# A trunk layer on one core: half steps in a fixed order per engine, and inner down projections in seven products

## The chip, the cores and the metric

One core of a Trainium2 chip runs the whole kernel in one launch. The metric is the device time of a run in microseconds (us); lower is better. TensorE (PE) multiplies, VectorE (DVE) and GpSimd (POOL) work elementwise, ScalarE (ACT) applies functions and copies, and SyncE (SP) issues all DMAs.

## The reference

One layer is run for 128 context tokens and 512 latent tokens (640 columns here) of width 1024, in fp32:

```
h = mod(rms_norm(x));  x += 1/2 * gate1 * (silu(h @ w_gate) * (h @ w_up)) @ w_down     (half step 1, d_ff 2816)
h = mod(rms_norm(x));  x += gate2 * ((g_a * fourier(h) + g_b * gla(h)) @ w_out)        (mixer)
h = mod(rms_norm(x));  x += 1/2 * gate3 * (silu(h @ w_gate) * (h @ w_up)) @ w_down     (half step 2)
```

The shifts, scales and gates come from silu(c) @ w_ada, with 9 x 1024 columns. The outputs are the normed x and the final states of the attention branch.

## The kernel before, in words

Activations lie with channels on the partitions, in pages of 128 x 2 x 640 (`page`, 29 buffers). For precision each operand of a large matmul is split in a high and a low part (`split`, lines 108 to 110: ACT copies the high part, DVE subtracts it for the low part), and each product is three matmuls (high x high, high x low, low x high).

A pair of output tiles (256 columns of a weight, all 640 tokens) is computed either plainly (`gemm_w`, 96 matmuls of 128 x 128 by 320 columns for 8 row tiles) or as a 2 x 2 block product with seven half-size products instead of eight (`Pair7`, 84 matmuls). `Pair7` needs sums of weight blocks, made by POOL in place (lines 522, 523, 538, 539), and sums of activation blocks, made once per activation (`Act7`). Its weights are split two blocks at a time (`double`, 1024 columns, for products 1+2, 7+5 and 6+3) and one alone (`single`, 512 columns, for product 4):

```
            if i in (1, 2):
                self.double(self.raw[:, :, 0:P], 1, 2, whole)
            elif i in (5, 7):
                self.weights(1)
                self.sums7()
                self.double(self.raw[:, self.ks[0], :], 7, 5, lambda j, o: (j, o * P))
```

Products 1, 2, 6, 5 and 7 of a pair run in `begin` and `end`; products 3 and 4 are held back (`held`) and run inside the next pair. What is done with a finished bank is a `Take` object's: `p1` and `p2` read the banks of products 1 and 2, `p16` reads the sum of 1 and 6, and so on.

A half step (`ffn`, lines 650 to 731) goes through the 22 hidden tiles in `PARTS` of 4, 6, 6 and 6: for each two hidden tiles f there is a gate pair and an up pair; after the first gate pair of the next part come the down projections of the part that is finished (`down`, plain, 8 output tiles; line 378 adds them to X). The last part's down projection runs in two halves of the tokens (`halved`, lines 382 to 424), so that the next norm, or the output, can begin. The first two hidden tiles are made plainly at the entry; the gate pair of the third and fourth is the first `Pair7`. In half step 1 the parts of w_ada for later stages are streamed in (`ada_stream`, 14 steps of four 512 KB loads and one small product each, `ada_fill` between pairs).

The program is traced in order, and a scheduler then orders each engine's instructions by a cost model of its own, within the dependencies. `pin(start)` (line 58) forbids that: it ties each instruction to the one before it on its engine. Before, the entry of a half step is pinned; the pairs after it are not. Buffers: `wraw` 2 (raw weights, 1 MB), `wspl2` 4 blocks of 1024 columns, `wspl` 2 blocks of 512, PSUM 6 banks for products. In the mixer, the gates (columns C_G of w_in), the Fourier inputs (C_F) and w_proj_gla are also `Pair7` pairs.

Of the kernel before, what the change touches and what calls it, by code (L numbers as in the profile page):

```python
# [34 lines left out]
def trunk_kernel(ctx: ExitStack, tc: tile.TileContext, I, O):  # L35
# [6 lines left out]
    wspl2 = ctx.enter_context(tc.tile_pool(name="wspl2", bufs=NBLK2))  # L42
# [54 lines left out]
    def sm_tile(shape, tag, dt=F32):  # L97
        uid[0] += 1
        return small.tile(shape, dt, tag=tag, name=f"{tag}{uid[0]}")
# [16 lines left out]
    def block2():  # L116
        uid[0] += 1
        return wspl2.tile([P, 2, 1024], F32R, tag="wspl2", name=f"wsplb{uid[0]}")

    def wsplit(src, new=block2, room=1024):  # L120
# [194 lines left out]
    class Norm:  # L315
# [27 lines left out]
        def spread(self, hf):  # L343
            rb = sm_tile([P, N], "t")[0:GB, 0:NG * P].rearrange("p (g c) -> p g c", g=NG)
# [36 lines left out]
    def halved(wd, r0, nk, acts, gate, X, each, mid, cut=NH):  # L381
# [22 lines left out]
        for hf, c0, c1 in ((0, 0, cut), (1, cut, N)):  # L404
            opened = []
            for mp in range(4):
                rd = load(wd, r0, nk, mp * 256, 256)
                for m in range(2):
                    w = wsplit(rd[:, :, m * P:(m + 1) * P])
                    ps = pb_ps()  # L410
                    if hf == 0 and mp < 2:
                        some(ps, w, c0, c1, range(nk - 2))
                        opened.append((2 * mp + m, ps, w))
                        flush_pair()
                        continue
# [8 lines left out]
    def even(h):  # L424
        return h[:, :, 0:NH]
# [51 lines left out]
    held = []  # L477

    def flush_step():
        if held:  # L480
            held.pop(0)()

    def flush_pair():
        while held:
            flush_step()

    class Pair7:
# [3 lines left out]

        def __init__(self, raw, act, take, alternate=False):
            n = self.n = raw.shape[1] // 2
            ks = (slice(0, 2 * n, 2), slice(1, 2 * n, 2)) if alternate else (slice(0, n), slice(n, 2 * n))
            self.ks, self.raw = ks, raw
            self.a11, self.a12, self.a21, self.a22 = [raw[:, k, c:c + P] for c in (0, P) for k in ks]
            self.act, self.take = act, take
            self.w, self.summed = {}, False

        def double(self, src, a, b, at):  # L500
            t = block2()[:, :, 0:2 * self.n * P]
            k, c = src.shape[1], src.shape[2]
# [12 lines left out]
        def early(self):
            self.single(1, self.a11)
            self.single(2, self.a12)
            self.sums7()

        def sums7(self):  # L520
            if not self.summed:
                G.tensor_tensor(out=self.a11, in0=self.a11, in1=self.a21, op=ALU.subtract)  # L522
                G.tensor_tensor(out=self.a21, in0=self.a21, in1=self.a22, op=ALU.add)  # L523
                self.summed = True

        def weights(self, i):
            if i in self.w:
                return
            whole = lambda j, o: (range(2 * self.n)[self.ks[o]][j], 0)
            if i in (1, 2):  # L530
                self.double(self.raw[:, :, 0:P], 1, 2, whole)
            elif i in (5, 7):
                self.weights(1)
                self.sums7()
                self.double(self.raw[:, self.ks[0], :], 7, 5, lambda j, o: (j, o * P))
            elif i in (6, 3):
                self.weights(7)
                G.tensor_tensor(out=self.a11, in0=self.a22, in1=self.a11, op=ALU.subtract)  # L538
# [930 lines left out]
```

## Time and profile before

| | |
|---|---|
| median of 3 runs | 1606.99 us (1605.3 to 1608.22) |
| profiled execution | 1608.41 us, span 1606.6 us |
| mean granted TensorE clock | 0.979 of full speed |
| PE, DVE, ACT, POOL busy | 94%, 62%, 43%, 26% of the span |
| DMA | 184.54 MB, mean 115 GB/s |

A row of a timeline is a run of instructions of one form: start, duration, engine, line, output<-inputs, shape, count; in brackets the idle time of the engine ahead of it and what ended it. A PE matmul is listed with its whole passage through the array, so the rate is read from a long row, not from the mean of one.

### The profile page before, as it was taken

What the parts mean: (1) busy time and instruction counts of PE and PEld (TensorE: products, weight loads), DVE (VectorE), ACT (ScalarE), POOL (GpSimd) and SP (SyncE); (2) the same over time, 40 slices, a digit from 0 to 9 for tenths busy, and PEclk for the clock granted to TensorE, in tenths of its full rate; (3) what the DMA queues carried; (4) which work ended last, traced back from release to release, by engine and by line L of the source; (5) the groups of instructions that cost most, each with busy time, mean ns of one, the idle gap of its engine ahead of it and who ended that gap; (6) DMA issues with size and microseconds to landing.
All of it is one profiled execution on the core that took longest, in us unless ns stands there. A gap on an engine that the chain in (4) does not pass through costs nothing. (4 is left out here: it accounts for less than half of the span.)

```text
span 1606.6 us, 27065 instructions
## 1 busy us (share of the span) xinstructions
PE 1508.0 (94%) x11162; PEld 1462.7 (91%) x11162; DVE 989.5 (62%) x1543; ACT 692.1 (43%) x1256; POOL 421.6 (26%) x324
## 2 busy tenths in 40 slices
PE   6789999999999899999799999899979999999998
PEld 5778999999999898999788999889979999999997
DVE  5744654465467766765866757577775564564566
ACT  5432342243254455454545444335543442442444
POOL 1411440341340000000333423430341431431420
PEclk8989999999999999999999999999999999999999
DMA  9265554422224512213124235364212222222223
GB/s 357 96 232 179 174 176 160 157 85 88 79 75 139 163 40 83 67 45 91 50 68 144 95 102 187 117 211 145 79 53 79 79 86 73 80 86 80 72 95 129
DMA packets 149330, 184.54 MB, mean 115 GB/s; under 512 B 4735, under 2 KB 121847, under 8 KB 149207
## 3 DMA queue, kind: packets, MB, share of 16 engines
q1 hardware_dynamic: 149207, 182.81, 34.4%
q8 instruction: 88, 1.44, 0.4%
q14 instruction: 35, 0.29, 0.1%
HBM read 168.64 MB, written 14.16 MB: 114 GB/s over the span
## 5 line engine op out<-in xcount | busy, mean ns | idle before, releaser
L550 PE MATMUL pb<-pg,wsplb 128*128 128x320 f32 x3744 | 583.3, 314 | 46.2 <-ACT hn L588 25.2
L550 PEld LDWEIGHTS pb<-pg,wsplb 128*128 128x128 f32 x3744 | 561.7, 191 | 58.6 <-ACT hn L588 26.2
L110 DVE TENSOR_TENSOR wsplb<-wraw,wsplb 128x1024 fp32r<-128x1024 f32 (+2 forms) x292 | 336.2, 1155 | 221.8 <-ACT wsplb L109 218.4
L109 ACT ACTIVATE wsplb<-wraw 128x1024 fp32r<-128x1024 f32 (+2 forms) x292 | 283.5, 975 | 426.1 <-PE pb L144 137.5
L144 PE MATMUL pb<-pg,wsplb 128*128 128x320 f32 x1920 | 287.7, 310 | 2.9 <-DVE pg L1301 2.1
L144 PEld LDWEIGHTS pb<-pg,wsplb 128*128 128x128 f32 x1920 | 282.8, 188 | 4.3 <-DVE pg L1301 2.3
L522 POOL TENSOR_TENSOR wraw<-wraw 128x512 f32<-128x512 f32 x53 | 70.8, 1335 | 486.8 <-DVE wsplb L110 465.0
L391 PE MATMUL pb<-pg,wsplb 128*128 128x320 f32 (+2 forms) x960 | 148.1, 313 | 3.7 <-DVE wsplb L110 3.4
L391 PEld LDWEIGHTS pb<-pg,wsplb 128*128 128x128 f32 x960 | 142.6, 190 | 4.4 <-DVE wsplb L110 3.6
L378 DVE SCALAR_TENSOR_TENSOR pg<-pb,hg,pg 128x320 f32<-128x320 f32 x144 | 54.5, 434 | 113.6 <-PE pb L144 113.6
L550 PE MATMUL pb<-pg,wspl 128*128 128x320 f32 x708 | 113.0, 309 | 0.0
L550 PEld LDWEIGHTS pb<-pg,wspl 128*128 128x128 f32 x708 | 106.1, 188 | 0.0
L538 POOL TENSOR_TENSOR wraw<-wraw 128x512 f32<-128x512 f32 x53 | 71.6, 1350 | 131.5 <-DVE wsplb L110 128.6
L917 PE MATMUL mm<-wsplb,pg 128*128 128x256 f32 x672 | 88.4, 288 | 0.0
L109 ACT ACTIVATE pg<-t 128x640 fp32r<-128x640 f32 (+1 forms) x56 | 41.0, 732 | 108.4 <-POOL t L647 61.9
L917 PEld LDWEIGHTS mm<-wsplb,pg 128*128 128x128 f32 x672 | 83.8, 195 | 0.4 <-ACT pg L1019 0.3
L539 POOL TENSOR_TENSOR wraw<-wraw 128x512 f32<-128x512 f32 x53 | 79.7, 1504 | 4.1
L110 DVE TENSOR_TENSOR wspl<-wraw,wspl 128x512 fp32r<-128x512 f32 x59 | 70.6, 1201 | 11.7 <-ACT wspl L109 11.6
L523 POOL TENSOR_TENSOR wraw<-wraw 128x512 f32<-128x512 f32 x53 | 71.3, 1344 | 3.1
L110 DVE TENSOR_TENSOR pg<-t,pg 128x640 fp32r<-128x640 f32 (+1 forms) x56 | 62.2, 1110 | 9.9 <-ACT pg L109 9.3
L110 DVE TENSOR_TENSOR pg<-pg,pg 128x320 fp32r<-128x320 f32 (+2 forms) x80 | 57.5, 767 | 6.5 <-ACT pg L109 6.5
L1120 POOL TENSOR_TENSOR rs<-ms,negh 128x5 f32<-128x5 f32 x4 | 4.7, 1174 | 212.4 <-DVE ms L1118 212.4
(217 smaller groups left out, 1700.1 us busy)
## 6 DMA issues: line engine op xcount, KB each, us to landing
pg<-in_w_ada_dram SPq DMA_DIRECT2D x72, 512.0 KB, 7.1
wraw<-in_w_ffn_down_dram SPq DMA_DIRECT2D x32, 768.0 KB, 4.5
wraw<-in_w_ffn_gate_dram SPq DMA_DIRECT2D x22, 1024.0 KB, 5.2
wraw<-in_w_ffn_up_dram SPq DMA_DIRECT2D x22, 1024.0 KB, 5.3
wraw<-in_w_in_dram SPq DMA_DIRECT2D x22, 512.0 KB, 3.7
wraw<-in_w_in_dram SPq DMA_DIRECT2D x10, 1024.0 KB, 5.1
wraw<-in_w_out_dram SPq DMA_DIRECT2D x8, 1024.0 KB, 5.3
gbd<-g SPq DMA_DIRECT2D x16, 320.0 KB, 2.4
```

The costliest lines, as they stand in the source:

```text
L109: S.activation(out=hi, in_=src, func=AF.Copy)
L110: eng.tensor_tensor(out=lo, in0=src, in1=hi.bitcast(F32), op=ALU.subtract)
L144: T.matmul(out=bank(ps, hf)[:, 0:NH], lhsT=w[a][k], rhs=acts[k][:, b, hf * NH:(hf + 1) * NH], start=(k == 0 and ti == 0), stop=(k == nk - ...
L378: V.scalar_tensor_tensor(out=X[k][:, a:b], in0=bank(ps, hf)[:, o:o + b - a], scalar=gate[:, k, r:r + 1], in1=X[k][:, a:b], op0=ALU.mult, o ...
L391: T.matmul(out=ps[:, 0:c1 - c0], lhsT=w[a][i], rhs=acts[i][:, b, c0:c1], start=(i == 0 and ti == 0), stop=(i == nk - 1 and ti == 2))
L522: G.tensor_tensor(out=self.a11, in0=self.a11, in1=self.a21, op=ALU.subtract)
L523: G.tensor_tensor(out=self.a21, in0=self.a21, in1=self.a22, op=ALU.add)
L538: G.tensor_tensor(out=self.a11, in0=self.a22, in1=self.a11, op=ALU.subtract)
L539: G.tensor_tensor(out=self.a12, in0=self.a12, in1=self.a11, op=ALU.subtract)
L550: T.matmul(out=bank, lhsT=self.w[i][s][k], rhs=x[k][:, t, :], start=first and k == 0 and ti == 0, stop=k == self.n - 1 and ti == 2, skip_g ...
L917: T.matmul(out=ps_out, lhsT=h2[k][:, a, t * P:(t + 1) * P], rhs=w[b][k], start=(k == 0 and ti == 0), stop=(k == KD - 1 and ti == 2))
L1120: G.tensor_tensor(out=rs[:, 0:TT], in0=ms[:, 0:TT], in1=negh[:, 0:TT], op=ALU.pow)
```

## The change

- Every weight block is split alone (512 columns or fewer, 9 blocks in `wspl`, `wspl2` gone), one product ahead of its use, by a list of steps (`STEPS`) that also holds the four POOL sums.
- `Pipe.stride` writes out one order for a pair j and the preparation of the next pair n; products 3 and 4 of the pair before run inside it. Small work on finished tiles is queued (`later`) and taken at five places (`pend`).
- The whole half step up to `halved` is pinned.
- The inner down projections are `Pair7` pairs too: the hidden tiles get the block sums (`Hidden7`), in place of plain splits. `TakeDown` adds the seven products' parts to X.
- Up pairs multiply each part by the gate as it comes (`TakeMul`), three of four on POOL.
- At the entries of both half steps and of the mixer's gates, one more pair is plain.
- The parts are (4, 6, 6, 6) in half step 1 and (6, 6, 6, 4) in half step 2.
- Of the 14 steps on w_ada, 8 move from half step 1 to the mixer, two after each of four strides there.

```diff
-NPAGES = 29
-NBLK = 2
-NBLK2 = 4
-M1, M2 = 2, 4
-PARTS = (4, 6, 6, 6)
+NPAGES = 30
+NBLK = 9
+PARTS1 = (4, 6, 6, 6)
+PARTS2 = (6, 6, 6, 4)
+DEEP = {"g": 4}
...
-    def wsplit(src, new=block2, room=1024):
+    def wsplit(src, new=block, room=512):
...
     class Pair7:
+        STEPS = (1, 2, "S3", "S1", 7, 5, "S2", 6, "S4", 3, 4)
...
+        def step(self, i, new):
+            if i == "S1":
+                G.tensor_tensor(out=self.a21, in0=self.a21, in1=self.a22, op=ALU.add)
+            elif i == "S2":
+                G.tensor_tensor(out=self.a11, in0=self.a22, in1=self.a11, op=ALU.subtract)
...
+            else:
+                src = {1: self.a11, 2: self.a12, 7: self.a11, 5: self.a21, 6: self.a11, 3: self.a12, 4: self.a22}[i]
+                t = new()[:, :, 0:self.n * P]
+                v = [t[:, s].rearrange("p (k c) -> p k c", k=self.n) for s in range(2)]
+                split(v[0], v[1], src)
...
+    class Pipe:
+        def stride(self, j, n=None, more=lambda: None, mid=lambda: None):
+            def ahead(step):
+                if n:
+                    n.prep(step)
+
+            j.A, C = pb_ps()[:, 0:NH], pb_ps()[:, 0:NH]
+            j.product(1, j.A, True)
+            j.take.p1(j.A)
+            self.pend()
+            j.prep("S4")
+            j.product(2, C, True)
+            j.take.p2(C)
+            j.prep(3)
+            self.tail3()
+            j.prep(4)
+            more()
+            ahead(1)
+            mid()
+            j.product(6, j.A, False)
+            j.take.p16(j.A)
+            self.pend()
+            ahead("S3")
+            j.B = pb_ps()[:, 0:NH]
+            j.product(5, j.B, True)
+            ahead(7)
+            self.tail4()
+            self.pend()
+            ahead(5)
+            j.product(7, j.A, False)
+            j.take.p167(j.A)
+            j.take.p5(j.B)
+            self.pend()
+            self.pend()
+            ahead(6)
+            self.prev = j
...
+    class TakeMul(Take):
+        def onto(self, part, i, hf):
+            x = self.into[i][:, hf * NH:(hf + 1) * NH]
+            return G.tensor_tensor(out=x, in0=x, in1=part, op=ALU.mult)
...
+        def p1674(self, ps):
+            x = self.into[1][:, 0:NH]
+            V.tensor_tensor(out=x, in0=ps, in1=x, op=ALU.mult)
+            self.done(1)
...
+    class Hidden7:
+        def first(self, x0):
+            def work():
+                G.tensor_tensor(out=x0[:, NH:N], in0=x0[:, NH:N], in1=x0[:, 0:NH], op=ALU.subtract)
+                h = self.put(x0)
...
+        def second(self, x1):
+            def raw():
+                h = self.put(x1)
...
+            def sums():
+                V.tensor_tensor(out=x1[:, NH:N], in0=x1[:, NH:N], in1=x0[:, NH:N], op=ALU.subtract)
+                V.tensor_tensor(out=x1[:, 0:NH], in0=x1[:, 0:NH], in1=x1[:, NH:N], op=ALU.subtract)
+                G.tensor_tensor(out=x0[:, 0:NH], in0=x1[:, NH:N], in1=x0[:, 0:NH], op=ALU.subtract)
+
+            def mixed():
+                h = self.put(x1)
...
+            pipe.later(raw, sums, mixed, third)
...
+    class TakeDown(TakeMul):
+        def onto(self, x, i, hf):
+            k = 2 * self.mp + i
+            for r, a, b in HSEG[hf]:
+                o = a - hf * NH
+                V.scalar_tensor_tensor(out=self.X[k][:, a:b], in0=x[:, o:o + b - a], scalar=self.gate[:, k, r:r + 1],
+                                       in1=self.X[k][:, a:b], op0=ALU.mult, op1=ALU.add)
...
     def ffn(hs, F, wg, wu, wd, gate, X, entry, each, mid, parts, fill=lambda: None, first=None, cut=NH):
+        for nf, hid in zip(parts, hids):
             for f in range(f0, f0 + nf, 2):
+                if f > 2:
+                    jobs.append(lambda f=f: gate_job(f))
+                jobs += downs
+                downs = []
+                if f > 0:
+                    jobs.append(lambda f=f, hid=hid: up_job(f, hid))
+            downs = [lambda f0=f0, nf=nf, hid=hid, mp=mp: down_job(f0, nf, hid, mp) for mp in range(KD // 2)]
+            f0 += nf
...
+        fill()
+        pipe.chain(jobs, one, two, fill)
+        pin(m1)
+        halved(wd, (DFF // P - parts[-1]) * P, parts[-1], hids[-1], gate, X, each, mid, cut)
...
-    stream = ada_stream((2, 4, 3, 5, 7, 6, 8))
-    quota = [2] + [1] * 16
+    stream = AdaStream((2, 4, 3))
+    quota = [2] + [1] * 4
...
+    stream = AdaStream((5, 7, 6, 8))
...
+    for _ in range(4):
+        pipe.stride(jobs[0], jobs[1], more)
+        jobs.pop(0)
+        two_steps()
```

## Rows read from the trace of the kernel before

**Rows 1.** The page's first part: busy time, share of the span, instructions.
```profile
PE 1508.0 (94%) x11162; PEld 1462.7 (91%) x11162; DVE 989.5 (62%) x1543; ACT 692.1 (43%) x1256; POOL 421.6 (26%) x324
```

**Rows 2.** Stretches: length, busy time of PE, PEld, DVE, ACT, POOL; clock, DMA share, GB/s.
```profile
100.00:150.00 50.00, 41.46 (x482) 37.45 (x481) 15.25 (x31) 11.61 (x19) 7.97 (x6) 0.90 0.79 283
...
1330.70:1367.70 37.00, 37.00 (x255) 37.00 (x254) 15.79 (x27) 7.43 (x9) 5.53 (x4) 1.00 0.28 87
1367.70:1393.20 25.50, 24.77 (x169) 24.51 (x168) 14.42 (x17) 10.52 (x15) 13.06 (x10) 1.00 0.21 69
1393.20:1419.15 25.95, 25.09 (x168) 24.66 (x168) 16.42 (x19) 12.51 (x21) 13.36 (x10) 1.00 0.26 81
```

**Rows 3.** The timeline of PE in half step 2: down tiles, and a pair.
```profile
1330.71 37.12 PE L144 MATMUL pb<-pg,wsplb 128*128 128x320 f32 x252
...
1393.26 5.54 PE L550 MATMUL pb<-pg,wsplb 128*128 128x320 f32 x36 [0.78 <-DVE g L602]
```

**Rows 4.** The timeline of PE at the entries of the stages.
```profile
81.31 16.41 PE L550 MATMUL pb<-pg,wsplb 128*128 128x320 f32 x92 [8.32 <-ACT hn L588]
...
113.06 1.96 PE L220 MATMUL sm<-pg,cs 128*32 128x128 f32 x64 [1.67 <-DMA pg<-in_w_ada_dram]
119.61 3.64 PE L220 MATMUL sm<-pg,cs 128*32 128x128 f32 x64 [4.59 <-DMA pg<-in_w_ada_dram]
...
868.78 7.08 PE L550 MATMUL pb<-pg,wsplb 128*128 128x320 f32 x36 [3.41 <-DVE g L602]
...
1021.26 16.78 PE L550 MATMUL pb<-pg,wsplb 128*128 128x320 f32 x96 [6.49 <-ACT hn L588]
...
1179.41 16.40 PE L550 MATMUL pb<-pg,wsplb 128*128 128x320 f32 x96 [8.10 <-ACT hn L588]
...
1207.36 0.56 PE L550 MATMUL pb<-pg,wsplb 128*128 128x320 f32 x2 [2.09 <-ACT wsplb L109]
```

**Rows 5.** The timeline of PE in the last down projection, first and second half.
```profile
1575.82 3.39 PE L391 MATMUL pb<-pg,wsplb 128*128 128x384 f32 x18
...
1588.89 2.40 PE L391 MATMUL pb<-pg,wsplb 128*128 128x256 f32 x18
```

**Rows 6.** The timeline of ACT, DVE and POOL in half step 2, in order of time.
```profile
1461.96 0.63 ACT L109 ACTIVATE wspl<-wraw 128x512 fp32r<-128x512 f32 x1 [0.96 <-DMA wraw<-in_w_ffn_up_dram]
1462.62 0.69 DVE L110 TENSOR_TENSOR wspl<-wraw,wspl 128x512 fp32r<-128x512 f32 x1 [0.64 <-ACT wspl L109]
...
1473.06 1.30 POOL L522 TENSOR_TENSOR wraw<-wraw 128x512 f32<-128x512 f32 x1 [37.18 <-DVE wsplb L110]
1473.31 1.59 DVE L110 TENSOR_TENSOR wspl<-wraw,wspl 128x512 fp32r<-128x512 f32 x1 [0.33 <-ACT wspl L109]
1474.43 1.62 POOL L523 TENSOR_TENSOR wraw<-wraw 128x512 f32<-128x512 f32 x1
...
1496.64 0.88 POOL L642 TENSOR_TENSOR t<-t,g 128x320 f32<-128x320 f32 x1
...
1504.07 0.74 ACT L109 ACTIVATE pg<-t 128x640 fp32r<-128x640 f32 x1 [4.19 <-POOL t L647]
```

**Rows 7.** Groups by line and form: busy us, mean ns of one, idle before.
```profile
L110 DVE TENSOR_TENSOR wspl<-wraw,wspl 128x512 fp32r<-128x512 f32 x59 | 70.6, 1201 | 11.7 <-ACT wspl L109 11.6
...
L1074 DVE TENSOR_TENSOR pg<-pg,pg 128x640 f32<-128x640 f32 x28 | 22.9, 818 | 0.0
...
L110 DVE TENSOR_TENSOR wsplb<-wraw,wsplb 128x512 fp32r<-128x512 f32 x24 | 17.3, 725 | 2.9 <-ACT wsplb L109 2.7
...
L602 DVE TENSOR_TENSOR g<-hn,pb 128x320 f32<-128x320 f32 x27 | 13.0, 480 | 5.2 <-ACT hn L599 5.1
...
L1375 DVE TENSOR_TENSOR pg<-pb,pg 128x128 f32<-128x128 f32 x40 | 9.7, 285 | 0.8 <-ACT junk L1372 0.6
...
L398 DVE SCALAR_TENSOR_TENSOR pg<-pb,hg,pg 128x128 f32<-128x128 f32 x24 | 7.8, 344 | 3.4 <-PE pb L391 3.3
```

**Rows 8.** DMA issues: count, KB each, median us from issue to landing.
```profile
pg<-in_w_ada_dram SPq DMA_DIRECT2D x72, 512.0 KB, 7.1
```

More of the change, by code (lines that the diff above doesn't have):

```diff
@@ L98, in sm_tile @@
         uid[0] += 1
[L99 removed]
+        return small.tile(shape, dt, tag=tag, name=f"{tag}{uid[0]}", bufs=DEEP.get(tag, 2))
     def load(w, r0, nk, c0, cols):
@@ L526, in weights @@
[L526 to L538, printed above, removed]
-                G.tensor_tensor(out=self.a12, in0=self.a12, in1=self.a11, op=ALU.subtract)
-                self.double(self.raw[:, :, 0:P], 6, 3, whole)
-            else:
-                self.single(4, self.a22)
+            self.w, self.steps = {}, list(self.STEPS)
@@ new lines, in chain, with make, finish @@
+        def chain(self, makers, first=None, second=None, between=lambda: None):
+            todo = list(makers)
+            def make():
+                return todo.pop(0)() if todo else None
+            jobs = [first or make(), second or make()]
+            while jobs[0]:
+                self.stride(jobs[0], jobs[1], lambda: jobs.append(make()))
+                jobs.pop(0)
+                between()
+        def finish(self):
+            self.tail3()
+            while self.pending:
+                self.pend()
+            self.tail4()
+            while self.pending:
+                self.pend()
+            self.prev = None
@@ new lines, in trunk_kernel, with first, work, p1 @@
+    class HiddenPlain(list):
+        def first(self, x):
+            def work():
+                h = page(F32R)
+                split(h[:, 0, :], h[:, 1, :], x)
+                self.append(h)
+            pipe.later(work)
+        second = first
+    class TakeUp(TakeMul):
+        def __init__(self, gate, hid):
+            self.g, self.hid = gate, hid
+        def p1(self, ps):
+            self.into = self.g.x0, self.g.x1
+            TakeMul.p1(self, ps)
+        def done(self, i):
+            (self.hid.second if i else self.hid.first)(self.into[i])
@@ new lines, in ffn @@
+        w = first
+        if w is None:
+            rg = load(wg, 0, KD, 0, 256)
+            ru = load(wu, 0, KD, 0, 256)
+            w = [wsplit(raw[:, :, i * P:(i + 1) * P]) for i in range(2) for raw in (rg, ru)]
+        p = [out_ps() for _ in range(3)]
+        raw = load(wg, 0, KD, 2 * P, 256)
+        one = jobs.pop(0)()
+        entry(p, w, one.early)
+        m1 = mark()
+        act = one.act = Act7(hs, paired(F))
+        act.each(act.sum13)
+        t0 = swiglu(p[0], p[1])
+        w2 = wsplit(raw[:, :, 0:P])
@@ new lines, in ffn @@
+        act.each(act.sum2)
+        p3 = out_ps()
+        gemm_w(p3, w[3], hs)
+        w3 = wsplit(raw[:, :, P:2 * P])
+        two = jobs.pop(0)()
+        act.each(act.put2)
+        t1 = swiglu(p[2], p3)
+        tg = gates[2]
+        tg.x0, tg.x1 = tg.out()
+        for x, v, work in ((tg.x0, w2, (7, 5, act.sum4, act.put3)), (tg.x1, w3, (6, act.put4))):
+            ps = out_ps()
+            gemm_w(ps, v, hs)
+            for i in work:
+                if isinstance(i, int):
+                    one.prep(i)
+                else:
+                    act.each(i)
+            for hf in range(2):
+                S.activation(out=x[:, hf * NH:(hf + 1) * NH], in_=bank(ps, hf)[:, 0:NH], func=AF.Silu)
```

401 lines of the change are left out of this document (169 added, 232 removed).

## The prediction

> **What bounds the kernel now.** I read the busy shares first: PE is busy for 94% of the span [rows 1], so time comes back only as fewer matmuls or less idle PE. Then the stretches: in half step 2 a down projection keeps PE busy throughout and leaves DVE and POOL more than half idle, while a gate and up pair take 25.5 to 25.95 us with DVE and POOL busy for 27 to 30 us together [rows 2]. So the stages differ: PE is full everywhere, but beside the pairs DVE and POOL are nearly full too. The timeline of PE gives the price of a matmul, 37.12 us for 252 or 0.147 us, and the small wait that the pairs have now, 0.78 us for DVE [rows 3]; nine such rows stand in the two half steps, some 7 us in all. The large idle times lie at the entries of the stages, each with a stretch behind it in which the same matmuls take longer [rows 4]: 92 matmuls in 16.41 us instead of 13.5.
>
> **Matmuls.** A plain down projection costs 48 matmuls for each hidden tile, as seven products 42. Half step 1 has 16 inner tiles, 768 becomes 672. Half step 2 has 16 inner and 6 last tiles, 768 + 288; now 18 and 4, 756 + 192. Three entries have one more plain pair, 96 for 84 each. The sum is -96 - 108 + 36 = -168 matmuls, at 0.147 us each -24.7 us. Not all of it arrives in the last projection: a tile of its second half now takes 2.40 us for 18 matmuls [rows 5] and would take 1.6 us for 12, but DVE has for each tile a split (0.69), two additions (0.34 each) and two products (0.29 each) [rows 6, 7], 1.95 us. I give back 0.33 x 8 = 2.6 us. **-22.1 us**, between -18 and -25.
>
> **Entries.** What is lost there now, idle time and slower matmuls against 0.147 us: half step 1: 8.32 + 2.9, then 1.67 + 4.59 for w_ada and 1.7 on the step behind it, 19.2 us; half step 2: 8.10 + 2.3 + 2.09, 12.5; mixer gates: 3.41 + 1.8, 5.2; w_proj_gla: 6.49 + 2.7, 9.2 [rows 4]. The two longest waits, of about 8 us, come since product 6 stands behind two double splits and all four POOL sums while PE has only two products to do. After the change PE has 96 more plain matmuls (14.1 us) at that point, which covers them; and with weights split alone product 6 of w_proj_gla needs fewer splits before it. What is late next: at the end of half step 1's entry two w_ada steps stand in fixed order, and the second can't be skipped by PE; its loads need pages that the first frees. A load takes 7.1 us to land [rows 8], so between 0 and 8.9 us (landing, and 1.8 us of slow clock); I take 7, since half its pages should be free earlier but the nearest row, 4.59 + 1.7 [rows 4], is this very wait. For the others I leave 2, 1.7 and 3.2 us. 46.1 - 13.9: **-32 us**, between -22 and -40.
>
> **w_ada in the mixer.** Eight steps (16.8 MB) and some five weight loads (5.2 MB) fall in four strides, 4 x 84 x 0.147 + 8 x 1.96 = 65 us of PE. At the 283 GB/s of the busiest such stretch [rows 2] they take 78 us. So 0 (the order is not pinned there, the scheduler may spread them) to 13 us; I take the lower middle, **+5 us**. The same steps leave half step 1, where 1.96 us each [rows 4] was PE's own work: no change in the sum.
>
> **The stride.** This is the large term. Per gate and up pair PE needs 168 x 0.147 = 24.7 us. DVE's low parts were six doubles and two singles; now they are 14 singles of 0.69 us [rows 6], 9.7 us. The hidden tiles, split twice before (0.82 each [rows 7]), are split three and a half times and take two subtractions: 3 x 0.82 + 0.48 + 0.96. DVE's additions from PSUM are 7 x 0.48 [rows 7]. POOL has the eight sums (1.30 each) and now five products or differences of 320 columns (0.88 each) [rows 6]: 14.8 us.
>
> What decides is how these two meet. A DVE split of 512 columns takes 0.69 us alone and 1.59 us when it begins inside a POOL sum; the next POOL sum takes 1.62 instead of 1.30 [rows 6]. The split that always came alone has a mean of 725 ns, the one beside POOL's work 1201 ns [rows 7]. So an operation with two SBUF inputs on DVE almost stands still until POOL's is through: from 1473.06 to 1476.05 us, 3.29 us of work was done in 2.99, an overlap of a tenth. DVE's share with two SBUF inputs (9.7 + 3.9 = 13.6 us) and POOL's 14.8 make 28.4 us per pair; with a tenth overlapped 25.8 us, 1.1 us more than PE needs, even if neither ever waits for anything else. Before, the two were busy for 27.5 to 29.8 us, work from PSUM and standing still included, and the pair took 25.5 to 25.95 [rows 2].
>
> The Trainium skill, "GPSIMD Engine Reference", section 2 (Architecture), puts it otherwise: POOL's two reads take turns on one SBUF read port that is shared with DVE. By that, turns could be taken element by element, some 22 us of port time would fit beside PE's 24.7, and this term would be near nothing; the row with 1.59 us speaks against it.
>
> Where it shows: ahead of product 6 of the up pair. From the end of the held product 4 in the gate stride, one chain runs in the new order: product with the gate 0.48, split of the raw tile 0.74 + 0.82, low part of 5 0.69, addition 0.48, first subtraction 0.48, POOL difference 0.88, S2 1.30, split of 6 0.63 + 0.69: 7.2 us. PE has products 7, 1, 2 and the held 3 meanwhile, 48 x 0.147 = 7.1 us. Without any meeting the wait is 0.1 us or so; if DVE stands still through S3, S1 and one POOL product before it, 3.5 us. I take 2.0, between the 1.1 of the count and the upper end. There are 12 such places (6 in each half step); ahead of a down stride (6 places) chain and cover both shrink by about a microsecond, so the same price: 18 x 2.0 = 36 us.
>
> A down stride of six tiles (20 of them) has 63 matmuls, 9.3 us, beside 7 splits of about 0.55, additions and updates of X of 3.9 us, and four sums of about 1.0 us (between the rows for 320 and 512 columns): 10 us of shared work with a tenth overlapped, 9.1 us. I take 0.2 us over (0 to 0.6). A stride of four tiles (4 of them) has 6.2 us of PE against 7.3: 1.0 us over (0.7 to 1.8). Together 8 us. The 7 us of waits that the pairs have now go. 36 + 8 - 7: **+37 us**, between 0 and +75.
>
> **Small splits elsewhere.** In the attention heads each split of 1024 columns becomes two, some 0.15 us more on DVE for each; PE is mostly the bound there: **+1 us**, 0 to 3. If PE were idle at those places it would be some 7 us.
>
> **Sum.** -22.1 - 32 + 5 + 37 + 1 = -11 us on the profiled execution's 1608.4 us, 1597.3; that execution lies 1.4 us above the median of the runs, so **1596 us**.
>
> **The rivals.**
>
> *The lock stays off the chain (faster, 1562 us).* If the meetings fall where DVE has slack, or turns are finer than the row shows, the 18 waits are 0.3 us and the stride term is 10 instead of 44: 1596 - 34. It is what the shared port of the Trainium skill's page would give. For it: the no-meeting chain fits almost exactly, and one downward end of the entries helps too. Against it: the split of 1.59 us [rows 6], and a count that exceeds PE's time.
>
> *The waits become long enough to slow the clock (slower, 1636 us).* Place: product 6 of each pair behind a gate stride. Gaps of 3.41 and 6.49 us are followed by matmuls at a lower rate, which cost 1.8 and 2.7 us [rows 4]; gaps of 0.78 us are not [rows 3]. At 3.0 us per place and half of them followed by 1.8 us, 18 x 3.9 + 14 = 84 us instead of 44: 1596 + 40. It decides from the point where the gap exceeds 2.6 us: 18 x 2.6 + 8 = 55 eats all the gains. For it: the fixed order forbids every engine to go round a late instruction, and DVE's 10.2 us and POOL's 8.7 us of a gate stride stand against 12.3 us of PE.
>
> *Gains and losses cancel (1607 us).* The w_ada loads take their 13 us and the entries keep a few more: 1596 + 8 + 3. Nothing excludes it; it needs several terms at once.
>
> **How the numbers follow.** Forecast (1580 to 1603, its own range) 0.38; lock off the chain 0.24; slow clock 0.28; cancelled 0.10. A difference of 0.2% (3.2 us) is about what a measurement of this kernel can tell from none. Faster 0.62, same 0.10, slower 0.28. The range takes in the middles of both outer cases: 1560 to 1638; a tenth lies beyond either end.
>
> **What would show it.** Right: pairs of about 26.5 to 27 us with PE waiting ahead of product 6 for ACT's copy or a low part of 6; DVE splits of 512 columns with a mean well above 0.69 us; POOL over 500 us busy; entries of half steps 1 and 2 without their 8 us gaps; a wait for w_ada at 85 to 92 us; a down part of six tiles at 38 to 40 us instead of 42. Wrong: pairs at 24.7 us (the lock costs nothing), a granted clock below 1.0 in the pairs (the second rival), or PE waits for w_ada of over 5 us in the mixer.

## The result and the profile after

The changed kernel takes 1635.5 us (median of 4 runs, 1634.39 to 1638.61) against 1607.6 us for the kernel before (4 runs too), a ratio of 1.018 (95% interval 1.016 to 1.020): slower by 28 us, where the prediction said 11 us faster. It lies inside the range, on the side to which a chance of 0.28 was given.

The first part of the page and, under it, TensorE's waits (line, what it waited for: us, times, longest). PE does less and is busy for a smaller share than in [rows 1]; DVE and POOL are busy for 196 and 176 us more.

```profile
PE 1513.0 (93%) x10994; PEld 1449.5 (89%) x10994; DVE 1185.5 (73%) x2001; ACT 793.1 (49%) x1687; POOL 597.2 (37%) x470
```

```profile
PE pb L516 <- ACT hn L657: 24.0, 15, 1.9
PE pb L516 <- DVE wspl L109: 14.7, 28, 0.8
PE pb L516 <- DVE g L620: 11.4, 16, 1.3
PE pb L516 <- DVE hn L664: 11.3, 12, 2.8
PE sm L215 <- DMA pg<-in_w_ada_dram: 7.9, 6, 3.7
PE pb L139 <- DVE pg L1431: 7.8, 2, 6.4
PE pb L516 <- ACT hn L606: 5.8, 7, 1.9
```

The four longest waits are for the helpers of the pairs: ACT's copy of product 1 (L657), the low part of a weight (L109) and the additions from PSUM (L620, L664). Stretch by stage, from the starts of TensorE's rows in both timelines (us):

| stage | before | after | difference |
|---|---|---|---|
| to the first plain pair of half step 1 | 62.3 | 60.2 | -2.1 |
| half step 1 up to the last projection | 427.4 | 424.1 | -3.3, though 15.6 us of w_ada steps and 12.3 us of matmuls left it |
| its last projection | 48.8 | 45.7 | -3.2 |
| attention heads | 300.2 | 289.5 | -10.7 |
| gates and Fourier part | 145.4 | 174.7 | +29.3, of which 17.4 us are w_ada steps and the plain pair |
| w_proj_fourier, w_proj_gla | 94.3 | 92.9 | -1.4 |
| w_out and norm | 81.9 | 83.3 | +1.4 |
| half step 2 up to the last projection | 392.0 | 423.2 | +31.3 |
| its last projection | 54.3 | 40.6 | -13.7 |

Here are four windows in the format of [rows 2]: a down part of six tiles, a pair of half step 2, the first matmuls behind a gap ahead of a down stride, and those behind a gap in a later pair. Then, in TensorE's timeline, the w_ada wait at the entry of half step 1, the gap ahead of the down stride, the pair, the gap in the later pair, and a tile of each half of the last projection (2.35 and 1.68 us for 12 matmuls, where [rows 5] have 3.39 and 2.40 for 18).

```profile
1254.85:1294.04 39.19, 38.62 (x251) 38.21 (x251) 32.36 (x60) 19.37 (x43) 20.35 (x16) 0.96 0.29 94
1319.87:1350.17 30.30, 25.96 (x169) 24.64 (x169) 20.86 (x28) 14.12 (x27) 16.86 (x13) 1.00 0.21 70
...
1254.85:1258.00 3.15, 3.15 (x12) 3.15 (x13) 1.94 (x5) 1.59 (x5) 0.00 (x0) 0.50 0.00 0
1484.40:1490.00 5.60, 5.45 (x20) 5.45 (x21) 4.05 (x8) 2.83 (x6) 1.62 (x2) 0.50 0.02 2
```

```profile
87.01 3.20 PE L215 MATMUL sm<-pg,cs 128*32 128x128 f32 x64 [3.66 <-DMA pg<-in_w_ada_dram]
...
1253.77 0.56 PE L516 MATMUL pb<-pg,wspl 128*128 128x320 f32 x2 [1.48 <-ACT hn L657]
1254.85 38.62 PE L516 MATMUL pb<-pg,wspl 128*128 128x320 f32 x250 [0.52 <-DVE wspl L109]
...
1319.87 2.02 PE L516 MATMUL pb<-pg,wspl 128*128 128x320 f32 x12 [0.79 <-DVE g L620]
1323.75 0.56 PE L516 MATMUL pb<-pg,wspl 128*128 128x320 f32 x2 [1.86 <-ACT hn L657]
1325.13 12.29 PE L516 MATMUL pb<-pg,wspl 128*128 128x320 f32 x82 [0.82 <-DVE wspl L109]
1337.94 0.56 PE L516 MATMUL pb<-pg,wspl 128*128 128x320 f32 x2 [0.53 <-ACT hn L606]
1338.86 10.53 PE L516 MATMUL pb<-pg,wspl 128*128 128x320 f32 x70 [0.36 <-DVE wspl L109]
1350.17 2.02 PE L516 MATMUL pb<-pg,wspl 128*128 128x320 f32 x12 [0.78 <-DVE g L620]
...
1483.18 0.58 PE L516 MATMUL pb<-pg,wspl 128*128 128x320 f32 x2 [1.86 <-ACT hn L657]
1484.56 24.75 PE L516 MATMUL pb<-pg,wspl 128*128 128x320 f32 x148 [0.79 <-DVE wspl L109]
...
1601.82 2.35 PE L386 MATMUL pb<-pg,wspl 128*128 128x384 f32 x12
...
1611.62 1.68 PE L386 MATMUL pb<-pg,wspl 128*128 128x256 f32 x12
```

A pair takes 30.30 us for 168 matmuls, which need 24.7; before it took 25.5 to 25.95 [rows 2]. The 5.6 us are lost at three kinds of places. Start to start, against 0.147 us a matmul, 3.2 us go ahead of the up pair's product 6 (1323.75 and 1325.13), 1.4 us ahead of the gate pair's (1337.94 and 1338.86), 1.0 us ahead of the held product 3 (1350.17). The clock is 1.00 throughout this pair, but not in all of them. It fell to 0.50 (1.2 GHz) for 3.4 to 6.9 us at ten places in the strides of the two half steps: behind the waits ahead of product 6 in 4 of 9 up pairs and 5 of 6 down strides, and once behind a wait of 2.08 us ahead of a product 3. Nearly the same waits, 1.86 and 0.8 us, were followed by 1.00 at 1325.13 and by 0.50 at 1484.56. The slower matmuls at the ten places cost about 17 us in all (start to start, against 0.147 us). The kernel before had a clock of 1.00 in all its pairs behind the entries.

What the helpers do meanwhile, from the timeline of all engines in that pair and the end of the next stride:

```profile
1319.73 0.48 DVE L719 TENSOR_TENSOR g<-g,g 128x320 f32<-128x320 f32 x1
...
1320.36 1.11 POOL L721 TENSOR_TENSOR g<-g,g 128x320 f32<-128x320 f32 x1 [4.73 <-DVE g L719]
...
1321.44 1.26 POOL L494 TENSOR_TENSOR wraw<-wraw 128x512 f32<-128x512 f32 x1
...
1322.74 0.63 ACT L108 ACTIVATE wspl<-wraw 128x512 fp32r<-128x512 f32 x1 [1.23 <-POOL wraw L494]
1322.79 1.74 POOL L498 TENSOR_TENSOR wraw<-wraw 128x512 f32<-128x512 f32 x1
1323.28 0.42 ACT L657 ACTIVATE hn<-pb 128x320 f32<-128x320 f32 x1
1323.40 1.67 DVE L109 TENSOR_TENSOR wspl<-wraw,wspl 128x512 fp32r<-128x512 f32 x1
...
1344.16 1.77 POOL L492 TENSOR_TENSOR wraw<-wraw 128x512 f32<-128x512 f32 x1
1344.70 2.39 DVE L109 TENSOR_TENSOR wspl<-wraw,wspl 128x512 fp32r<-128x512 f32 x2
1347.01 0.48 DVE L679 TENSOR_TENSOR g<-pb,g 128x320 f32<-128x320 f32 x1
```

Read it backwards. Product 6 waits for ACT's copy of product 1 (L657); that is queued behind the split of 6, which waits for S2 (L494) on POOL; S2 is written behind the hidden tile's difference (L721), which needs DVE's subtraction (L719). This chain begins with the product with the gate (L679). TensorE ends the held product 4 for it at 1338.86 + 34 x 0.147 = 1343.9, but DVE comes to it at 1347.01, since low parts are written ahead of it and take 2.39 us for two beside POOL's S1 (L492).

### The profile page after: what moved, and what is told of

Its sections match the earlier page's. It is cut to its first block, busy times and chain, and to the rows that moved or that the text cites. A ratio compares the mean times of both kernels' runs of the same rounds, so it can differ in the third digit from the quotient of the medians.

```text
span 1634.2 us, 27775 instructions
## 1 busy us (share of the span) xinstructions
PE 1513.0 (93%) x10994; PEld 1449.5 (89%) x10994; DVE 1185.5 (73%) x2001; ACT 793.1 (49%) x1687; POOL 597.2 (37%) x470
## 4 chain that ended last, share of the span: by engine, by line
PE 41%; DVE 29%; POOL 11%; ACT 8%; issue 7%; DMA 4%; SPq 2%; POOLq 0%; ACTq 0%; DVEq 0%
DVE wspl L109 13%; PE pb L516 10%; PE pb L386 6%; PE pb L139 5%; DVE pg L109 5%; PE mm L1035 5%; POOL wraw L496 4%; ACT wspl L108 3%; ACT pg L108 3%; POOL g L661 3%; PE mm L139 2%; DMA pg<-in_w_ada_dram 2%; PE sc L1184 2%; DVE pg L769 2%; DVE hn L664 2%
## 5 line engine op out<-in xcount | busy, mean ns | idle before, releaser
L516 PE MATMUL pb<-pg,wspl 128*128 128x320 f32 x5556 | 867.5, 316 | 72.9 <-ACT hn L657 24.0
L516 PEld LDWEIGHTS pb<-pg,wspl 128*128 128x128 f32 x5556 | 835.5, 192 | 101.7 <-ACT hn L657 27.9
L109 DVE TENSOR_TENSOR wspl<-wraw,wspl 128x512 fp32r<-128x512 f32 (+2 forms) x676 | 550.4, 833 | 206.1 <-ACT wspl L108 203.6
L108 ACT ACTIVATE wspl<-wraw 128x512 fp32r<-128x512 f32 (+2 forms) x676 | 382.0, 589 | 324.3 <-POOL wraw L496 94.6
L496 POOL TENSOR_TENSOR wraw<-wraw 128x512 f32<-128x512 f32 (+2 forms) x74 | 112.7, 1523 | 231.5 <-DVE wspl L109 218.8
L386 PE MATMUL pb<-pg,wspl 128*128 128x320 f32 (+2 forms) x864 | 132.6, 311 | 1.7 <-DVE wspl L109 1.6
L109 DVE TENSOR_TENSOR pg<-g,pg 128x640 fp32r<-128x640 f32 (+1 forms) x90 | 90.5, 1007 | 58.1 <-ACT pg L108 57.8
L386 PEld LDWEIGHTS pb<-pg,wspl 128*128 128x128 f32 x864 | 127.2, 188 | 2.4 <-DVE wspl L109 1.9
L108 ACT ACTIVATE pg<-g 128x640 fp32r<-128x640 f32 (+1 forms) x90 | 61.3, 682 | 125.2 <-DVE g L679 47.3
L139 PE MATMUL pb<-pg,wspl 128*128 128x320 f32 x672 | 106.1, 317 | 7.9 <-DVE pg L1431 7.8
L139 PEld LDWEIGHTS pb<-pg,wspl 128*128 128x128 f32 x672 | 102.1, 193 | 9.3 <-DVE pg L1431 8.5
L494 POOL TENSOR_TENSOR wraw<-wraw 128x512 f32<-128x512 f32 (+2 forms) x74 | 89.8, 1213 | 50.1 <-DVE wspl L109 50.1
L498 POOL TENSOR_TENSOR wraw<-wraw 128x512 f32<-128x512 f32 (+2 forms) x74 | 105.1, 1421 | 5.6
L492 POOL TENSOR_TENSOR wraw<-wraw 128x512 f32<-128x512 f32 (+2 forms) x74 | 101.9, 1377 | 5.8
L1035 PE MATMUL mm<-wspl,pg 128*128 128x256 f32 x672 | 87.4, 286 | 0.1
L1035 PEld LDWEIGHTS mm<-wspl,pg 128*128 128x128 f32 x672 | 82.4, 191 | 0.5 <-ACT pg L1137 0.3
L109 DVE TENSOR_TENSOR pg<-pg,pg 128x320 fp32r<-128x320 f32 (+2 forms) x80 | 57.1, 762 | 9.4 <-ACT pg L108 9.4
L131 PE MATMUL pb<-pg,wspl 128*128 128x320 f32 x288 | 48.0, 320 | 4.3 <-DVE pg L366 1.9
```

Source lines behind the costliest of these rows:

```text
L108: S.activation(out=hi, in_=src, func=AF.Copy)
L109: eng.tensor_tensor(out=lo, in0=src, in1=hi.bitcast(F32), op=ALU.subtract)
L131: T.matmul(out=bank(ps, hf)[:, 0:NH], lhsT=w[a][k], rhs=acts[k][:, b, hf * NH:(hf + 1) * NH], start=(k == 0 and ti == 0), stop=(k == nk - ...
L139: T.matmul(out=bank(ps, hf)[:, 0:NH], lhsT=w[a][k], rhs=acts[k][:, b, hf * NH:(hf + 1) * NH], start=(k == 0 and ti == 0), stop=(k == nk - ...
L386: T.matmul(out=ps[:, 0:c1 - c0], lhsT=w[a][i], rhs=acts[i][:, b, c0:c1], start=(i == 0 and ti == 0), stop=(i == nk - 1 and ti == 2))
L498: G.tensor_tensor(out=self.a12, in0=self.a12, in1=self.a11, op=ALU.subtract)
```

## The experiments

Two theories. **Lock** (theory A in the expectations): DVE operations with two SBUF inputs wait for POOL's, so their sum is the bound. **Order** (theory B): on each engine the written order puts an instruction that TensorE needs behind one that is late. An engine is *tied* where its instructions are pinned to the written order. E1 to E18 are the first parts of the labels. In diffs V is DVE and G is POOL.

| run | edit (on the changed kernel) | us | ratio to before (95%) |
|---|---|---|---|
| | the change itself | 1635.5 | 1.018 (1.016 to 1.020) |
| E1 | S2 and the split of 6 written earlier | 1648.6 | 1.026 (1.022 to 1.029) |
| E2 | sums on DVE | 1609.3 | 1.002 (1.000 to 1.003) |
| E3 | pairs not tied | 1580.8 | 0.984 (0.981 to 0.987) |
| E4 | E1 + E2 | 1619.7 | 1.007 (1.005 to 1.010) |
| E5 | E2 + E3 | 1517.8 | 0.945 (0.943 to 0.948) |
| E6 | split of 6 behind the copy | 1637.4 | 1.020 (1.017 to 1.023) |
| E8 | plain inner downs | 1600.4 | 0.996 (0.995 to 0.998) |
| E9 | E2 + E6 | 1605.7 | 0.999 (0.998 to 1.001) |
| E10 | E2, DVE alone not tied | 1547.2 | 0.964 (0.961 to 0.967) |
| E11 | E2, ACT alone not tied | 1601.4 | 0.997 (0.995 to 0.999) |
| E12 | E5 + plain inner downs | 1547.4 | 0.964 (0.961 to 0.966) |
| E13 | S2 alone written earlier | 1616.9 | 1.007 (1.005 to 1.009) |
| E14 | E2 + E13 | 1581.7 | 0.984 (0.982 to 0.986) |
| E16 | w_ada steps spread | 1620.9 | 1.009 (1.007 to 1.011) |
| E17 | E5 + E16 | 1509.8 | 0.939 (0.938 to 0.941) |
| E18 | E17, POOL's pair work on DVE | 1503.5 | 0.936 (0.935 to 0.938) |

**E7, the lock by itself.**

> Computes nothing of the layer: DVE low parts (512 columns, two SBUF inputs), POOL subtractions (512 columns) and DVE additions with one input in PSUM (320 columns), each alone and then side by side, and POOL beside ACT copies; only the durations count. Theory A: low part 0.69 us alone, 1.3 us or more beside POOL, so that DVE does little more than one of them per POOL operation (8 POOL operations of 1.3 to 1.6 us take 8 to 11 low parts along); the PSUM additions keep 0.48 us. If the slow low parts of the kernel had another cause (late inputs counted as busy), 0.69 us in both.

Timeline: DVE alone, POOL alone, both, PSUM additions alone and beside POOL.

```profile
5.85 5.77 DVE L64 TENSOR_TENSOR lo<-a,hi 128x512 fp32r<-128x512 f32 x8
13.64 10.64 POOL L60 TENSOR_TENSOR gz<-a,b 128x512 f32<-128x512 f32 x8
...
26.43 13.44 POOL L60 TENSOR_TENSOR gz<-a,b 128x512 f32<-128x512 f32 x8
26.99 13.42 DVE L64 TENSOR_TENSOR lo<-a,hi 128x512 fp32r<-128x512 f32 x8
...
48.20 8.32 DVE L77 TENSOR_TENSOR vz<-b,ps 128x320 f32<-128x320 f32 x16 [1.37 <-POOL gz L56]
...
58.68 12.49 DVE L81 TENSOR_TENSOR vz<-b,ps 128x320 f32<-128x320 f32 x24 [1.44 <-POOL gz L56]
58.72 10.68 POOL L60 TENSOR_TENSOR gz<-a,b 128x512 f32<-128x512 f32 x8
```

As the lock theory expected. A low part takes 0.72 us from start to start and a POOL operation 1.33; side by side they go one for one, 8 and 8 in 13.4 us, 1.68 us for one of each. One after the other they would take 2.05 us. So 2.05 us of work is done in 1.68, an overlap of 22% by the prediction's own count (3.29 us in 2.99, a tenth). An addition with one input in PSUM keeps its 0.52 us, and POOL beside it its 1.33.

The Trainium skill, "SBUF — State Buffer", section "Who interferes with whom", says that a DVE instruction with two SBUF inputs contends with a GpSimd instruction that reads SBUF, and that one with at most one SBUF input, outside the 2-port modes, does not. This run agrees, with 1.68 us for one of each against 0.52 unchanged. The same page of the Trainium skill, section "Terms", says that the loser of the shared port pair blocks fully for the whole instruction; here 0.37 us of the two run together.

**E2, E3, E5: lock and order, one at a time and both.**

```
E2:  - G.tensor_tensor(out=self.a21, ...)   + V.tensor_tensor(out=self.a21, ...)      (S1; likewise S2, S3, S4)
E3:  - fill(); pipe.chain(jobs, one, two, fill); pin(m1)
     + pin(m1); fill(); pipe.chain(jobs, one, two, fill)
```

> Edit: the four sums of weight blocks of each pair (S1 to S4) on DVE instead of POOL; order as in the changed kernel. Theory A (lock): the low parts of 512 columns fall back to about 0.7 us (mean of the group from 833 to about 640 ns), a sum costs DVE 0.7 us in place of 1.3 to 1.7 us of POOL in which DVE stood still, pairs at 26 to 28 us, 1580 to 1610 us. Theory C (DVE's amount of work is the bound, no lock): eight sums of 0.7 us are added to each pair on the busiest helper, pairs at 31 us or more, 1640 to 1680 us. Theory B (order) expects a small gain at most, by the 0.6 us that S2 itself is shorter: 1615 to 1635 us.

> Edit: the instructions of the pairs and inner down projections of both half steps are no longer tied to the written order on their engine; the entry stays tied. Theory B: the scheduler takes S2 and the split of 6 ahead of late work, waits ahead of product 6 shrink by half, 1590 to 1615 us. Theory A: DVE's and POOL's sum is as before, 1625 to 1645 us. If the written order is better than the scheduler's, slower than 1645 us.

> Edits of e3_pairs_not_pinned (1580.8 us) and e2_sums_on_dve (1609.3 us, 26 us under the changed kernel) together. If the written order and the lock are two separate losses: 1580.8 - 20 to 26, 1555 to 1562 us, low parts at 0.69 us. If the scheduler's order already keeps DVE and POOL apart where it matters, the sums only load DVE: 1578 to 1590 us.

E2 gains 26 us and ends at the slow end of the lock theory's band: the mean of the 512-column low parts falls from 880 to 739 ns, yet TensorE still waits 39.3 us for ACT's copy. E3 gains 55 us, 9 more than the order theory's band allows, though the low parts are as slow as before. The groups by line and form of the changed kernel, E2 and E3, and E2's longest wait:

```profile
L109 DVE TENSOR_TENSOR wspl<-wraw,wspl 128x512 fp32r<-128x512 f32 x492 | 423.9, 880 | 177.8 <-ACT wspl L108 175.8
```

```profile
L109 DVE TENSOR_TENSOR wspl<-wraw,wspl 128x512 fp32r<-128x512 f32 x492 | 356.0, 739 | 125.2 <-ACT wspl L108 122.3 <-PE pb L516 2.0
```

```profile
L109 DVE TENSOR_TENSOR wspl<-wraw,wspl 128x512 fp32r<-128x512 f32 x492 | 432.9, 895 | 126.2 <-ACT wspl L108 123.9
```

```profile
PE pb L516 <- ACT hn L657: 39.3, 34, 2.1
```

So neither theory alone holds. E3 shows that part of the loss is order alone; E5 against E3 shows that the sums on POOL cost 63 us in the scheduler's order too. E5 gains 118 us, 37 more than the two separately (26 + 55), and lies 37 us below its own band: with both gone nothing in the pairs is late, and the clock stays at 1.00 in both half steps behind the entry of the first. What the 26 and 63 us consist of is not shown: a sum on DVE ends the meetings, but it is also shorter (0.7 us for 1.3), and no run separates the two. TensorE's timeline in half step 2, 1854 matmuls without a wait, 0.147 us each:

```profile
1147.77 272.40 PE L516 MATMUL pb<-pg,wspl 128*128 128x320 f32 x1854 [0.36 <-ACT sqh L613]
```

**E1, E4, E6, E9: the split of 6 moved.**

```
E1:    ahead(5)
     + ahead(6)                  # S2 and the split of 6
       j.product(7, j.A, False)
       ...
     - ahead(6)
E6:    j.take.p1(j.A)
     + j.prep(6)
       ...
     - ahead(6)
     + ahead("S2")
```

> Edit: in the stride, the sum S2 and the split of product 6 of the next pair are put ahead of product 7 of this pair instead of at the stride's end. Theory A (the lock: DVE operations with two SBUF inputs stand still beside POOL's, so their sum is the bound): the same work meets elsewhere, pairs stay at 29.5 to 30.5 us, 1620 to 1640 us. Theory B (the written order: S2 and split 6 stand behind this pair's additions, hidden sums and POOL products, so product 6 comes late by the chain): the waits ahead of product 6, 2.7 us behind a gate stride and 0.9 us behind an up stride, go; pairs at 26 to 27 us, 1575 to 1595 us.

> Edits of e1_six_early and e2_sums_on_dve together. Theory A alone true: as e2 (1580 to 1610 us), the early place adds under 5 us. Theory B alone true: as e1 (1575 to 1595 us). Both true: about 1560 us, pairs at 25.0 to 25.5 us with no wait above 0.3 us ahead of product 6.

> Edit: sums on POOL and written order as in the changed kernel, but the split of product 6 is queued behind ACT's copy of product 1 in the next stride instead of ahead of it (S2 stays where it was). Theory B in its narrow form (ACT's copy of product 1 is late only since it is queued behind a split that waits for S2): the 24 us of waits for that copy at product 6 go, those for the low part of 6 grow by at most the 0.4 us of the copy; pairs at 28.5 us, 1605 to 1618 us. Theory A (S2 itself comes late, since DVE and POOL are late in sum): the wait turns into one for the low part of 6, same length, 1630 to 1645 us.

> Edits of e2_sums_on_dve (1609.3 us) and e6_six_after_copy together, written order kept. In e2 the largest wait left is TensorE's for ACT's copy of product 1 (39 us), which stands behind the split of 6. If the place of that split in ACT's order is what is left: 1570 to 1585 us. If, as in e6 with the sums on POOL, S2 itself is late, the wait turns into one for the low part of 6: 1600 to 1612 us.

E1 is a miss, 13 us slower: neither theory named that. The waits at product 6 go, but the low part of 6 now stands on DVE ahead of this pair's addition (L664), for which the held product 3 waits. From E1's waits:

```profile
PE pb L516 <- DVE hn L664: 59.4, 35, 3.8
PE pb L516 <- DVE g L620: 16.6, 15, 1.9
```

E4 missed all its bands as well, for the same reason (35.1 us for L664). In E6 the wait for the copy turned into waits for the two halves of the split of 6 (23.9 and 22.6 us) and the time stayed: S2 itself is late, and the copy named last in the trace was not the cause. E9 says the same with the sums on DVE (1605.7 against 1609.3).

**E10, E11: whose order.** From E2 on, one engine at a time is left untied in the pairs.

```
-  def pin(start):                                        +  def pin(start, free=()):
-      for i in nc.cur_bb.bb.instructions[start:]:        +      for i in [i for i in ...[start:] if i.engine not in free]:
-  fill(); pipe.chain(jobs, one, two, fill); pin(m1)      +  pin(m1); fill(); m3 = mark(); pipe.chain(...); pin(m3, (DVE,))
```

> Sums on DVE; in the pairs only DVE is free of the written order (TensorE, ACT, POOL and the DMA queue keep it). From 1609.3 us with all tied and 1517.8 us with none. If the place of S2 in DVE's order is the cause (behind the hidden tiles' sums and splits): 1520 to 1545 us. If ACT's order is: 1595 to 1612 us.

> Sums on DVE; in the pairs only ACT is free of the written order. If ACT's order is the cause (its copy of product 1 stands behind the split of 6): 1520 to 1545 us. If DVE's order is: 1590 to 1612 us. If both are needed: both this and e10 above 1560 us.

DVE's order it is, though E10 ends 2 us above its band: 62 of the 91 us between E2 and E5, against 8 for ACT's. S2 (L494) in E2 and in E10, with the product with the gate (L679) of the same stride:

```profile
1326.42 0.48 DVE L679 TENSOR_TENSOR g<-pb,g 128x320 f32<-128x320 f32 x1
...
1332.01 0.68 DVE L494 TENSOR_TENSOR wraw<-wraw 128x512 f32<-128x512 f32 x1
```

```profile
1280.55 0.69 DVE L494 TENSOR_TENSOR wraw<-wraw 128x512 f32<-128x512 f32 x1
1281.16 0.49 DVE L679 TENSOR_TENSOR g<-pb,g 128x320 f32<-128x320 f32 x1
```

As written, S2 comes 5.6 us after that product, behind the whole chain of the hidden tile; the scheduler puts it ahead.

**E13, E14: S2 alone.**

```
-  ahead(5)
+  ahead(5), ahead("S2")
   j.product(7, j.A, False)
```

> The changed kernel, sums on POOL, all tied to the written order; one instruction per stride is written elsewhere: S2 right behind the split of 5, ahead of product 7, and the split of 6 stays at the stride's end (e1 had moved both). If S2's place is what made the pairs late: the waits ahead of product 6 go as far as the lock lets them, towards the 1580.8 us of e3: 1585 to 1610 us. If what e10 gained came from other moves on DVE: 1620 to 1640 us.

> The same move with the four sums on DVE, all tied. If S2's place is the cause: from 1609.3 us to near e10's 1547 us, 1540 to 1565 us. If not: 1595 to 1612 us.

One instruction per stride, written earlier, gains 18.6 us with POOL's sums and 27.6 with DVE's. That is a real part of the loss, but each lies above its band (1616.9 against 1610, 1581.7 against 1565). In E14 the largest wait is the next one in line, 17.7 us for the addition L620 ahead of product 3. So S2's place is less than half of the 62 us that DVE's order costs. Which other moves make up the rest between E14 and E10 (35 us) was not taken apart.

**E8, E12: the inner downs plain again.** Pairs as in the change; `HiddenPlain` for every part and two plain products per down stride in place of a `Pair7`.

> Undoes one part: the inner down projections are plain again (48 matmuls for a hidden tile instead of 42, 204 more in all), hidden tiles split once, without block sums; all else as in the changed kernel, the written order too. By the prediction's own terms: +30 us of matmuls, -8 us of down strides, -3 to -8 us in the pairs for the hidden sums that go: 1645 to 1655 us. If the hidden tiles' extra work is what makes the pairs late (theory A in its strongest form), pairs fall by 2.5 us or more and the two cancel: 1620 to 1640 us.

> The kernel of e5_not_pinned_and_dve (1517.8 us) with the plain inner down projections of e8. With the pairs no longer late, 204 matmuls of 0.147 us should show in full: +30 us less what little the pairs still wait, 1540 to 1550 us. If seven products pay nothing even then: under 1525 us.

In the tied kernel 204 more matmuls make it 35 us faster, below both bands of E8: without the hidden sums a pair takes 26.3 us instead of 30.3. In E12, where nothing is late, the same edit costs 29.6 us against 204 x 0.147 = 30.0. The seven products were worth what was predicted, and the helpers' work that they bring cost 65 us in this order. TensorE's row of a whole pair in E8:

```profile
1302.24 25.05 PE L516 MATMUL pb<-pg,wspl 128*128 128x320 f32 x168 [1.29 <-DVE g L653]
```

**E15, E16: heads and w_ada.** E15 is the kernel before with `split` called on halves of 512 columns in `wsplit`. E16 puts one step after each of the first four strides of the mixer and two after each of the next four.

> The kernel before, with each plain weight block of 1024 columns split in two halves of 512 (same buffers). Asked: where the 10.7 us that the attention heads gained come from. If from the finer splits (weights ready earlier): heads at 290 to 294 us instead of 300.2, about 1597 us. If from buffers or the scheduler's new order: heads within 2 us of 300, or moved with no relation to the splits; 1603 to 1610 us. By the prediction's term: +1 us.

> The changed kernel; of the eight w_ada steps in the mixer one follows each of the first four strides and two each of the four strides with the Fourier part's token products (two after each of the first four, before), so that 283 GB/s need not be passed. If the bunching is what cost about 12 us there: the stretch from the gates to the Fourier part 8 to 12 us shorter, 1623 to 1628 us. If the loads are hidden and other waits (additions of the pairs) are the cost: within 3 us of 1635.5.

E15 took 1597.2 us (ratio 0.995, 0.993 to 0.997), the number expected of finer splits, but not at the expected place. The heads took 297.5 us (532.51 to 830.02), 2.7 less, and kept their longest wait of 4.7 us; 6 us came earlier, up to the end of half step 1. So 8 of the heads' 10.7 us are not from the splits. Buffers or the scheduler's order may be; that was not tried. E16 gained 14.6 us, 2 more than its band, the stretch of the gates 11.4 of them (163.3 instead of 174.7), the wait behind it (L1431) 3.6. The clock there went from 0.97 to 1.00 at 216 instead of 202 GB/s, so the loads fit when they are spread.

**E17, E18: together.**

```
E18:  - return G.tensor_tensor(out=x, in0=x, in1=part, op=ALU.mult)
      + return V.tensor_tensor(out=x, in0=x, in1=part, op=ALU.mult)      (and the two differences in Hidden7)
```

> Sums on DVE, pairs not tied (e5, 1517.8 us), and the w_ada steps of the mixer spread over eight strides (e16, 14.6 us under the changed kernel). If the three are separate losses: 1503 to 1508 us. If the scheduler had already spread the loads once the sums left POOL: 1512 to 1520 us.

> As e17, and POOL's products with the gate and differences of hidden tiles go to DVE too, so that POOL does nothing in the pairs. Lock theory carried on: each of them costs DVE 0.5 us in place of 0.9 to 1.2 us in which it can be held, up to 5 us faster than e17. If TensorE is full already: within 3 us of e17. If DVE's amount of work binds now (81% busy in e5): slower than e17 by over 3 us.

E17 is 8 us under E5, 2 us above its band, so half of the spreading's gain is left. E18 takes 6.3 us more away, a little above the forecast of up to 5, with DVE busy for 82% and POOL for 5% of the span. It is the fastest of all, 6.4% under the kernel before (ratio 0.936). TensorE's row in half step 2:

```profile
1129.78 325.18 PE L516 MATMUL pb<-pg,wspl 128*128 128x320 f32 x2216
```

## Why the prediction was wrong, step by step

| term | predicted | measured |
|---|---|---|
| matmuls | -22.1 | -24.7 by count and price; nothing had to be given back |
| entries | -32 | about -18 |
| w_ada in the mixer | +5 | about +17 |
| stride | +37 | about +69 |
| small splits (heads) | +1 | -11, of which the splits are 2.7 (E15) |
| sum | -11 | about +32; stretches without a term gave 4 back, and the spans differ by +27.6 |

**The step that failed is the stride term.** It priced one wait for each gate stride, ahead of the next product 6, and put the rest at nothing. Against 0.147 us a matmul the strides lost 93 us in all (45.7 and 47.7 in the two half steps) where 44 were forecast. Start to start, the 93 us are:

- about 36 us ahead of product 6 behind a gate stride (L657, and the low part behind it). That is the 36 us forecast, but by luck: 13 places of 2.7 us instead of 18 of 2.0. The chain stands in 15 of the 18 places, since the last part's hidden tiles get no block sums, and two of the 15 are counted at the entries here.
- about 21 us for additions ahead of the held product 3 (L620, L664), and 6 us ahead of the gate pair's product 6 (L606), where S2 stands behind POOL's product with the gate. Apart from 8 us for the down strides the prediction had no price for them.
- about 17 us of matmuls at a clock of 0.50, which the sum left to a rival.
- some 13 us in small pieces.

Before, the strides lost about 24 us (32.2 and 23.9 in the two half steps, less 19.2 and 12.5 at the entries), not the 7 of the waits alone.

In the mechanism, the sentence "Without any meeting the wait is 0.1 us or so" is wrong. It let the chain of 7.2 us begin when TensorE ends the held product 4. In the trace DVE comes to it 3.1 us later (1347.01 against 1343.9), and the price of 2.0 us became 3.2 in a pair. E2 has no sums on POOL and still waits 2.1 us at this place:

```profile
1304.96 23.28 PE L516 MATMUL pb<-pg,wspl 128*128 128x320 f32 x156 [2.12 <-ACT hn L657]
```

There the held product 4 ends at 1304.96 + 120 x 0.147 = 1322.6, and DVE comes to L679 at 1326.42, 3.8 us later, with the low parts and now S3 and S1 written ahead of it. E10 shows what DVE's order costs in all: with it alone untied, 62 us come back.

**The lock** was seen at the right place with the right sign. Its size was off the other way: by E7 the overlap is 22%, not a tenth. With that the 28.4 us of shared work would take 23.3 us (an estimate), less than TensorE's 24.7, and the count alone would have given no wait. E3 shows what the count could not: with low parts as slow as before (895 ns), another order is 55 us faster.

**Matmuls**: right; E12 shows the price to 0.4 us. The last tiles take 1.68 us for 12 matmuls of 256 columns, so DVE's 1.95 us was overestimated and the give-back did not come.

**Entries**: the two 8 us gaps of [rows 4] went, but 11.4 and 8.4 us stay lost in half steps 1 and 2, where 7 and 2 were left over; the mixer's gates lose next to nothing at their entry. At w_proj_gla the wait of 6.49 us is gone, but w_proj_fourier ahead of it waits 6.41 us for L1431 (2.06 at this place before), so that the two together, 522 matmuls both times, gained only 1.4 of the 9.2 us. That is about 27.6 left of 46.1, where 13.9 were forecast, and outside the bounds of -22 to -40. The w_ada wait at 87.01 us is 3.66 us and 64 matmuls behind it take 3.20 instead of 1.95. The rest are small waits of the fixed order (1.2 to 1.9 us for L606, L657 and L664), which the prediction did not see at the entries.

**w_ada**: the stretch of the gates and the Fourier part is 12 us longer than its steps and its plain pair explain, although 5.2 us were gained at its entry. So the term is about +17, above its bounds of 0 to 13. E16 gives 14.6 us back by spreading the steps, so bunching is most of it.

**The rivals.** The second one came within a microsecond (1636), and its mechanism was there: the waits ahead of product 6 in a pair pass 2.6 us (1.86 and 0.82), and the clock fell at 9 of 15 such places, where it reckoned with half. All ten falls cost some 17 us, where it had 14. What it lacks are the waits at the other places. That its total agrees is partly luck, since the entries, w_ada and the heads were off by 14, 12 and -12 us. The first rival needed meetings where DVE has slack, or finer turns of the port. In the written order the meetings did not fall where DVE has slack. E7 shows more overlap than the rows did (1.68 us for one operation of each, where the sum is 2.05); whether the turns are whole operations it does not show. Of the signs, the six-tile down part (39.2 us), POOL's 597 us, the wait at 87 us and the low parts' mean came as written. The pairs at 26.5 to 27 us did not: 30.3. Of the signs of being wrong, a clock below 1.0 in the pairs came, in 4 of 9.

## What to carry to other kernels

When a chain of helper work is priced against the time that TensorE covers, start it when its first engine is free by the new order, not when its input is ready. Count every instruction written ahead of it there. A written order on the busiest helper is worth testing by untying one engine at a time: here, with the sums on DVE, DVE's order alone cost 62 us and ACT's 8. Count what a wait does to the clock as well: ten falls cost 17 us here beside the waits themselves. And sums with both inputs in SBUF were better on DVE here, where DVE otherwise stood beside POOL: 0.7 us of its own work replaced 1.3 us or more of POOL's, and gave 26 us in the tied order and 63 in the free one.

## Unexpected

Two losses that hide each other add to more than their sum: 26 and 55 us singly, 118 together. And an optimisation can be right and still cost time: 204 fewer matmuls made the tied kernel 35 us slower and the free one 29.6 us faster.
